# A two-block transformer on one core: attention scores of the first block in float32, or as a split into two float32r passes

## Chip, cores and metric

The kernel runs on one core of one Trainium2 chip. The metric is the device time of one execution in microseconds, the median of several runs.

## The reference, cut to what matters

The input is 256 tokens of width 1024. The first block has four layers: layer 0 and 3 use mixer A (16 query heads on 4 key heads, window 128, biases, sinks), layer 1 uses mixer B (three dilation groups of 16 heads each, merged by their softmax sums), layer 2 uses mixer C (16 heads, causal). Each layer is a mixer, an output projection, a layer norm, a gated feed-forward part and another layer norm. A second block of two layers follows (spatial gating, a state-space mixer, differential attention), which the change leaves as it is. All of it is float32. The scores of the first block come from

```python
s = jnp.einsum('bnqhgd,bnkhd->bnhgqk', qb, kb) * (dh ** -0.5)
...
m = s.max(-1)
p = jnp.exp(s - m[..., None])
l = p.sum(-1)
o = jnp.einsum('bnhgqk,bnkhd->bnqhgd', p, vb) / ...
```

with heads of 64 elements and blocks of 128 tokens; a query sees its own block and the one before it.

## The kernel before

The 256 tokens are two tiles of 128, and each tile is a *stream*: a Python generator that issues the projections of all layers in order. Beside the stream a tile has *tasks* (the attention of a finished projection, a hidden chunk of the feed-forward part), of which up to three advance at a time (`CONC`). `run` gives stream 0 a turn, then stream 1, which lags four turns (`LAG`). A turn lets each task go to its next `yield` and then issues one half unit of weights of the stream: two row blocks of the weights, three products each, so six products of 512 columns. `idle(n)` in a task waits n turns. This order and the dependences are all that orders the instructions on an engine; each engine works its own queue in order.

Every weight matrix is split: `load` fetches it (DMA on SP's queue), ScalarE makes the high part by a cast to float32r (line 396), VectorE the rest by a subtraction (line 400). `mm3` (lines 409 to 411) adds three float32r products: high by high, high by low, low by high. Activations are split in the same way after their transposes by TensorE (`blocks_t`, line 456; `split`, lines 447 and 448).

A projection chunk of 512 columns in layers 1 and 2 holds two blocks of 256 columns, that is four heads of queries, keys or values. `after` copies a block from PSUM to `stg` (line 765), rotates it (`rope_apply`, lines 581 to 584), and `heads_t` transposes it by TensorE and copies the result to SBUF by ScalarE (line 590). Then, a turn later, `attend` runs for the four heads: `scores` issues float32 products with 64 rows of contraction, two heads of different parity alternating between the upper and the lower 64 rows (line 614); VectorE adds the mask (lines 618 and 621) and finds the maxima (line 636), ScalarE takes exponentials (line 641); two turns later TensorE transposes them (line 664), and a turn after that come the products with the values (line 652). Layers 0 and 3 do the same in `keys` and `queries`; there each key head serves four query heads, and `keys` doubles the keys (line 711) so that both parities find them in their own 64 rows.

The first block calls `attend` 24 times for each token tile: 4 in each of layers 0, 2 and 3, 12 in layer 1. It handles 24 tiles of 256 query columns and 18 of key columns for each token tile. Tile 0 has 128 keys per head, tile 1 has 256. The second block's differential attention calls `scores` too.

`BUFS` gives the number of buffers of each kind of tile: here `tp` two PSUM banks for transposes, `v` values, `kt` and `qt` transposed keys and queries, `stg1` staged blocks, `ffg` the gates of the feed-forward part.

Of the kernel before, what the change touches and what calls it, by code (L numbers as in the profile page):

```python
# [9 lines left out]
F32 = mybir.dt.float32  # L10
# [57 lines left out]
W_QK_A = 1  # L68
W_QK_B = 0
W_SOFTMAX = 2  # L70
# [14 lines left out]
class Net:  # L85
# [45 lines left out]
    def own(self, name, shape, tag, dt=F32):  # L131

        if tag in ("s4", "yt", "lv", "cc", "cv", "xc", "sscb", "ssbt", "ssact"):
            self.second_pool()
        pp = self.pl if tag in ("ho", "wx", "yt") else self.pp
        return pp.tile([P] + shape, dt, name=name, tag=tag, bufs=BUFS[tag])
# [466 lines left out]

    def scores(self, t, q, k, mask):

        nc = self.nc
        nk = (t + 1) * P
        svs = [self.bank().rearrange("p (h k) -> p h k", k=256)[:, :, :nk] for _ in range(2)]  # L610
        for a in range(2):
            for j in range(t + 1):
                for par in range(2):
                    nc.tensor.matmul(svs[par][:, a, j * P:(j + 1) * P], q(par, a), k(par, a, j), start=True, stop=True)  # L614
        for sv in svs:
            if mask is None:
                m = self.mask["b0"][:, None, P:].to_broadcast([P, 2, P])
                nc.vector.tensor_add(sv[:, :, t * P:], sv[:, :, t * P:], m)
            else:
                m = mask[:, None, (1 - t) * P:].to_broadcast([P, 2, nk])  # L620
                nc.vector.tensor_add(sv, sv, m)
        return svs

    def attend(self, t, qt, kt, mask, v, sink=None):
# [6 lines left out]

        svs = self.scores(t, lambda par, a: qt[par * 64:par * 64 + 64, a, :],
                          lambda par, a, j: kt(j, par + 2 * a), mask)
        for par, sv in enumerate(svs):
# [50 lines left out]
    def mixer_a(self, t, i, xt, st):  # L685
# [13 lines left out]
        def keys(ps):  # L699
# [6 lines left out]
            self.rope_apply(z, 4, self.rope[1][t])  # L706

            k2 = []
            for a in range(2):
                k = self.own("k2", [2, 2, 64], "stg1")  # L710
                nc.vector.tensor_copy(k, z[:, 128 * a:128 * a + 128].rearrange("p (h d) -> p h d", d=64)[:, :, None, :]
                                      .to_broadcast([P, 2, 2, 64]))
                k2.append(k.rearrange("p h a d -> p (h a d)"))
            yield from self.idle(W_QK_A)
            st["k", t] = [self.heads_t(k, "kt", 1.0) for k in k2]

        def queries(c, ps):
# [7 lines left out]
            yield from self.idle(W_QK_A)  # L725
            qts = [self.heads_t(z, "qt", 0.125) for z in zs]
            yield
            def head(a):
                kvh = 2 * c + a
                h0 = 4 * kvh  # L730
                while ("k", 0) not in st:
                    yield
                o, nm = yield from self.attend(
                    t, qts[a], lambda jj, h: st["k", jj][kvh // 2][(h % 2) * 64:(h % 2) * 64 + 64, kvh % 2, :],
                    self.mask["a"], lambda jj, h: st["v", jj][:, kvh, :], nsk[:, h0:h0 + 4])
# [13 lines left out]
    def mixer_bc(self, t, i, xt, st, blocks, masks):  # L749
# [7 lines left out]
        def after(bl, ps):  # L757
# [12 lines left out]
            for z, what, qq, g in zs:  # L770
                if what == "k":
                    st["k", qq, g, t] = self.heads_t(z, "kt", 1.0)
                else:
                    qs.append((self.heads_t(z, "qt", 0.125), qq, g))
            if not qs:
                return
            yield
            for zt, qq, g in qs:
                while any((a, qq, g, j) not in st for a in "kv" for j in range(t + 1)):
                    yield  # L780
                o, nm = yield from self.attend(
                    t, zt, lambda j, h: st["k", qq, g, j][(h % 2) * 64:(h % 2) * 64 + 64, h // 2, :],
                    masks[g] and self.mask[masks[g]], lambda j, h: st["v", qq, g, j][:, h, :])
# [351 lines left out]
    def diff_attn(self, t, pr, st):  # L1135
# [7 lines left out]
        for hp in range(2):  # L1143
            ps, ls = [], []

            svs = self.scores(t, lambda m, a: qt[64 * m:64 * m + 64, 2 * hp + a, :],
                              lambda m, a, j: st["dk", j][64 * m:64 * m + 64, 2 * hp + a, :], None)
            for sv in svs:
# [374 lines left out]
```

## Time and profile before

| | us |
|---|---|
| median of 3 runs | 2391.38 |
| lowest and highest | 2390.16, 2392.42 |
| the profiled execution | 2393.47 |
| its span, first to last instruction | 2391.8 |
| TensorE busy | 2358.1 |
| VectorE busy | 1744.3 |
| ScalarE busy | 1314.9 |
| GpSimd busy | 124.7 |

PE is TensorE's products, PEld its weight loads, DVE VectorE, ACT ScalarE, POOL GpSimd, SP the engine that issues most DMAs. Products are pipelined: a record of a product lasts longer than its share of the engine (a product of 512 columns shows 0.39 us, but the next starts 0.23 us after it), so what a product costs is read from the steps in the chain or from the starts in the order of time. A line number can be that of a helper that many callers use. The granted clock of TensorE was at its full level (1.00, that is 2.4 GHz) in all four attention stretches.

### The profile page before, as it was taken

What the parts mean: (1) busy time and instruction counts of PE and PEld (TensorE: products, weight loads), DVE (VectorE), ACT (ScalarE), POOL (GpSimd) and SP (SyncE); (2) the same over time, 40 slices, a digit from 0 to 9 for tenths busy, and PEclk for the clock granted to TensorE, in tenths of its full rate; (3) what the DMA queues carried; (4) which work ended last, traced back from release to release, by engine and by line L of the source; (5) the groups of instructions that cost most, each with busy time, mean ns of one, the idle gap of its engine ahead of it and who ended that gap; (6) DMA issues with size and microseconds to landing.
All of it is one profiled execution on the core that took longest, in us unless ns stands there. A gap on an engine that the chain in (4) does not pass through costs nothing.

```text
span 2391.8 us, 34975 instructions
## 1 busy us (share of the span) xinstructions
PE 2358.1 (99%) x11664; PEld 1922.7 (80%) x11664; DVE 1744.3 (73%) x4282; ACT 1314.9 (55%) x2180; POOL 124.7 (5%) x411
## 2 busy tenths in 40 slices
PE   8999999999999999999999999999999999999999
PEld 6888888888888788887788877877888778788887
DVE  7765676666755767557775588987877889987876
ACT  5454456655544555444544445744677657545776
POOL 1000000000000000000000000100011201000111
PEclk9999999999999999999999999999999999999999
DMA  6366554444566635665366567467566686575653
GB/s 234 100 207 187 176 176 131 135 128 128 182 188 187 192 124 173 191 187 184 112 193 191 186 134 168 127 150 203 161 191 186 170 186 128 123 216 171 187 184 115
DMA packets 280117, 400.16 MB, mean 167 GB/s; under 512 B 20588, under 2 KB 205098, under 8 KB 279936
## 3 DMA queue, kind: packets, MB, share of 16 engines
q1 hardware_dynamic: 274784, 381.88, 55.4%
q0 software_dynamic: 5152, 16.05, 2.2%
q8 instruction: 92, 1.51, 0.3%
q14 instruction: 89, 0.73, 0.1%
HBM read 396.81 MB, written 1.05 MB: 166 GB/s over the span
## 4 chain that ended last, share of the span: by engine, by line
PE 87%; DVE 7%; DMA 3%; ACT 2%; issue 1%; SPq 0%; ACTq 0%; DVEq 0%
PE pj L409 21%; PE pj L411 21%; PE pj L410 21%; PE tp L456 4%; PE ch L409 4%; PE ch L411 4%; PE ch L410 4%; PE ch L614 3%; PE ch L652 3%; DVE w L400 2%; DMA raw<-in_w_in_dram 2%; PE tp L664 1%; ACT w L396 1%; DVE convy L1003 1%; DMA raw<-in_w_branch_c_dram 0%
## 5 line engine op out<-in xcount | busy, mean ns | idle before, releaser
L400 DVE TENSOR_TENSOR w<-raw,w 128x512 fp32r<-128x512 f32 x1456 | 956.3, 683 | 456.6 <-ACT w L396 455.1
L396 ACT CAST w<-raw 128x1024 fp32r<-128x1024 f32 x728 | 759.0, 1043 | 661.5 <-PE pj L411 361.0
L409 PE MATMUL pj<-w,xth 128*128 128x512 f32 x2048 | 821.7, 402 | 4.3 <-ACT w L396 1.6
L410 PE MATMUL pj<-w,xth 128*128 128x512 f32 x2048 | 806.1, 394 | 2.9 <-DVE w L400 2.9
L411 PE MATMUL pj<-w,xtl 128*128 128x512 f32 x2048 | 805.1, 394 | 0.7 <-DVE xtl L448 0.7
L409 PEld LDWEIGHTS pj<-w,xth 128*128 128x128 f32 x2048 | 386.4, 189 | 89.3 <-ACT xth L447 5.7
L411 PEld LDWEIGHTS pj<-w,xtl 128*128 128x128 f32 x2048 | 386.3, 189 | 85.4 <-DVE xtl L448 3.0
L410 PEld LDWEIGHTS pj<-w,xth 128*128 128x128 f32 x2048 | 386.9, 189 | 80.6 <-DVE w L400 5.3
L409 PE MATMUL ch<-w,fht 128*128 128x512 f32 x412 | 171.9, 417 | 1.8 <-ACT fht L447 1.8
L411 PE MATMUL ch<-w,fht 128*128 128x512 f32 x412 | 161.9, 393 | 0.0
L410 PE MATMUL ch<-w,fht 128*128 128x512 f32 x412 | 161.2, 391 | 0.0
L1003 DVE SCALAR_TENSOR_TENSOR convy<-xc,ffn_cw,convy 128x128 f32<-128x128 f32 x352 | 100.5, 345 | 7.1 <-POOL ffn_hist L994 2.1
L411 PEld LDWEIGHTS ch<-w,fht 128*128 128x128 f32 x412 | 77.3, 188 | 18.4 <-DVE fht L448 1.0
L409 PEld LDWEIGHTS ch<-w,fht 128*128 128x128 f32 x412 | 77.4, 188 | 15.5 <-ACT fht L447 3.9
L410 PEld LDWEIGHTS ch<-w,fht 128*128 128x128 f32 x412 | 77.9, 189 | 12.2
L641 ACT ACTIVATE pexp<-ch,nm 128x128 f32<-128x128 f32 (+1 forms) x192 | 65.9, 421 | 36.8 <-DVE nm L636 24.0
L845 ACT ACTIVATE ffg<-pj 128x256 f32<-128x256 f32 x88 | 33.9, 386 | 76.1 <-PE pj L411 76.0
L1000 ACT ACTIVATE convy<-xc,ffn_cw 128x128 f32<-128x128 f32 x176 | 72.8, 484 | 1.4
L652 PEld LDWEIGHTS ch<-v,pt 128*128 128x128 f32 x576 | 70.6, 191 | 2.9
L409 PE MATMUL pj<-w,fht 128*128 128x512 f32 x180 | 71.3, 396 | 0.0
L411 PE MATMUL pj<-w,fht 128*128 128x512 f32 x180 | 70.7, 393 | 0.0
L410 PE MATMUL pj<-w,fht 128*128 128x512 f32 x180 | 70.1, 389 | 0.0
(338 smaller groups left out, 2706.2 us busy)
## 6 DMA issues: line engine op xcount, KB each, us to landing
raw<-in_w_gate_up_dram SPq DMA_DIRECT2D x352, 256.0 KB, 3.3
raw<-in_w_in_dram SPq DMA_DIRECT2D x128, 512.0 KB, 5.0
raw<-in_w_down_dram SPq DMA_DIRECT2D x88, 512.0 KB, 3.6
raw<-in_ffn_w_up_dram SPq DMA_DIRECT2D x176, 256.0 KB, 3.3
raw<-in_b_w_qkv_dram SPq DMA_DIRECT2D x144, 256.0 KB, 3.1
raw<-in_ffn_w_down_dram SPq DMA_DIRECT2D x44, 512.0 KB, 4.4
raw<-in_a_w_qkv_dram SPq DMA_DIRECT2D x24, 512.0 KB, 4.5
raw<-in_c_w_qkv_dram SPq DMA_DIRECT2D x48, 256.0 KB, 3.1
```

Of the source, the lines that this page charges most:

```text
L396: nc.scalar.copy(w[:, 0, :m], raw)
L400: self.last_low = nc.vector.tensor_sub(w[:, 1, s], raw[:, s], w[:, 0, s].bitcast(F32)).ins
L409: mm(ps, xh[:, k, :], wh[:, kk, cols], start=start, stop=False)
L410: mm(ps, xh[:, k, :], wl[:, kk, cols], start=False, stop=False)
L411: self.last_mm = mm(ps, xl[:, k, :], wh[:, kk, cols], start=False, stop=stop).ins
L456: self.nc.tensor.transpose(tp[:, b * P:(b + 1) * P], src[:, b * P:(b + 1) * P], self.ident)
L614: nc.tensor.matmul(svs[par][:, a, j * P:(j + 1) * P], q(par, a), k(par, a, j), start=True, stop=True)
L641: nc.scalar.activation(p[:, a, :(t + 1) * P], sv[:, a, :], AF.Exp, bias=n2[:, a:a + 1])
L652: nc.tensor.matmul(o[:, par + 2 * a, :], pts[par][:, a * (t + 1) + j, :], v(j, par + 2 * a), start=j == 0, stop=j == t)
L845: nc.scalar.activation(g, ps[:, :FFC], AF.Silu)
L1000: nc.scalar.activation(y[:, a, :], xc[:, a, 4:], AF.Identity, bias=b[:, 0, c:c + 1], scale=w[:, h, c:c + 1])
L1003: nc.vector.scalar_tensor_tensor(y[:, a, :], xc[:, a, o:o + P], w[:, j, c:c + 1], y[:, a, :], op0=OP.mult, op1=OP.add)
```

## The change

The scores of the first block no longer multiply float32 operands of 64 rows. Queries and keys are split into a float32r high part and a float32r rest. A query tile holds the high part in the 64 rows of its head's parity and the rest in the other 64 rows; a key tile holds, for each parity, the high part in all 128 rows (`part` 0) and the rest in all 128 rows (`part` 1). One product over 128 rows then adds (high + rest of the query) times one part of the key, and two passes give the score. The high parts are written by ScalarE, the rests by VectorE, which writes the queries' rest across to the other 64 rows; for keys GpSimd copies both parts across. A key tile is shared by both token tiles, so a pass of token tile 1 takes 256 key columns at once. The doubled keys of layers 0 and 3 are no longer made by VectorE and transposed.

The scores are issued two turns after the transposes of their queries instead of one (`W_SPLIT`), in layers 1 and 2 the transposes a turn after the rotation instead of at once (`W_QK_B`), and in layer 1 the blocks come in the order keys, values, queries instead of values, keys, queries. Buffers: `v` 6 for 7; `ks` 2 and `qs` 3 in place of `kt` 5 and `qt` 3; `stg1` 6 takes in `ffg`. The second block keeps the old products under the name `scores_64`.

```diff
-            bc=3, bcs=1, v=7, kt=5, qt=3, stg1=2, og=7, ob=3, ffg=4,
+            bc=3, bcs=1, v=6, ks=2, qs=3, stg1=6, og=7, ob=3,
...
-W_QK_B = 0
+W_QK_B = 1
+W_SPLIT = 2
...
-                for w in (2, 1, 0):
+                for w in (1, 2, 0):
...
-    def heads_t(self, z, tag, scale):
-
+    def queries_t(self, z, scale):
+        nc = self.nc
         tp = self.blocks_t(z, 2)
-        zt = self.own("zt", [2, P], tag)
-        self.nc.scalar.activation(zt, tp, AF.Copy, scale=scale)
+        zt = self.own("zt", [2, 2, P], "qs", F32R)
+        for par in range(2):
+            here, there = self.half(par), self.half(1 - par)
+            nc.scalar.activation(zt[here, par], tp[here], AF.Copy, scale=scale)
+            nc.vector.scalar_tensor_tensor(zt[there, par], tp[here], scale, zt[here, par].bitcast(F32),
+                                           op0=OP.mult, op1=OP.subtract)
         return zt
+
+    def keys_t(self, z, ks, j):
+        nc = self.nc
+        tp = self.blocks_t(z, 2)
+        s = slice(j * P, (j + 1) * P)
+        for par in range(2):
+            here, there = self.half(par), self.half(1 - par)
+            nc.scalar.copy(ks[here, 0, par, :, s], tp[here])
+            nc.vector.tensor_sub(ks[here, 1, par, :, s], tp[here], ks[here, 0, par, :, s].bitcast(F32))
+            nc.gpsimd.tensor_copy(ks[there, :, par, :, s], ks[here, :, par, :, s])
...
+    def key_pair(self):
+        return self.own("ks", [2, 2, 2, 2 * P], "ks", F32R)
...
+    def scores(self, t, q, k, mask):
+        svs = self.score_banks(t)
+        for par, sv in enumerate(svs):
+            for a in range(2):
+                for part in range(2):
+                    self.nc.tensor.matmul(sv[:, a, :], q(par, a), k(par, a)[:, part, :(t + 1) * P],
+                                          start=part == 0, stop=part == 1)
+        return self.masked(t, svs, mask)
...
-            k2 = []
-            for a in range(2):
-                k = self.own("k2", [2, 2, 64], "stg1")
-                nc.vector.tensor_copy(k, z[:, 128 * a:128 * a + 128].rearrange("p (h d) -> p h d", d=64)[:, :, None, :]
-                                      .to_broadcast([P, 2, 2, 64]))
-                k2.append(k.rearrange("p h a d -> p (h a d)"))
             yield from self.idle(W_QK_A)
-            st["k", t] = [self.heads_t(k, "kt", 1.0) for k in k2]
+            self.keys_t(z, self.shared((i, "ks"), self.key_pair), t)
...
-            qts = [self.heads_t(z, "qt", 0.125) for z in zs]
-            yield
+            qts = [self.queries_t(z, 0.125) for z in zs]
+            yield from self.idle(W_SPLIT)
...
-                    st["k", qq, g, t] = self.heads_t(z, "kt", 1.0)
+                    self.keys_t(z, self.shared((i, "ks", qq, g), self.key_pair), t)
...
-                    qs.append((self.heads_t(z, "qt", 0.125), qq, g))
+                    qs.append((self.queries_t(z, 0.125), qq, g))
...
-            yield
+            yield from self.idle(W_SPLIT)
...
-        g = self.own("ffg", [FFC], "ffg")
+        g = self.own("ffg", [FFC], "stg1")
```

## Rows read from the trace of the kernel before

**Rows 1.** The page, part 1: busy time, share of the span, instructions.

```profile
PE 2358.1 (99%) x11664; PEld 1922.7 (80%) x11664; DVE 1744.3 (73%) x4282; ACT 1314.9 (55%) x2180; POOL 124.7 (5%) x411
```

**Rows 2.** The page, part 4: the chain that ended last, by engine.

```profile
PE 87%; DVE 7%; DMA 3%; ACT 2%; issue 1%; SPq 0%; ACTq 0%; DVEq 0%
```

**Rows 3.** Busy time by stretch: length, engines, PEclk, DMA share, GB/s.

```profile
30.00:100.00 70.00, 67.47 (x419) 54.84 (x417) 54.27 (x166) 39.30 (x88) 3.13 (x8) 1.00 0.41 129
...
300.00:620.00 320.00, 319.70 (x1835) 262.89 (x1835) 221.50 (x603) 185.68 (x391) 3.67 (x26) 1.00 0.45 137
...
815.00:925.00 110.00, 109.96 (x633) 90.64 (x632) 72.55 (x193) 65.18 (x128) 0.59 (x4) 1.00 0.44 137
...
1125.00:1195.00 70.00, 69.67 (x409) 55.28 (x407) 56.27 (x167) 40.02 (x89) 1.59 (x3) 1.00 0.40 131
```

**Rows 4.** TensorE's waits in 300 to 620 us: total, times, longest.

```profile
PE pj L411 <- DVE ho L448: 0.3, 1, 0.3
```

**Rows 5.** The chain by lines, for 30:100, 300:620, 815:925 and 1125:1195.

```profile
by line: PE ch L614 15.6%; PE ch L652 14.6%; PE pj L409 11.7%; PE pj L411 10.9%; PE pj L410 10.7%; PE tp L664 7.7%; PE tp L456 5.2%; DVE w L400 4.7%; ACT pexp L641 3.1%; ACT w L396 3.0%; issue 2.9%; DVE x L857 1.6%; PE ch L409 1.3%; PE ch L
...
by line: PE pj L409 23.9%; PE pj L411 22.5%; PE pj L410 22.1%; PE ch L652 9.6%; PE ch L614 7.8%; PE tp L664 4.9%; PE tp L456 4.3%; DMA raw<-in_w_gate_up_dram 1.2%; DVE w L400 0.6%; DVE x L553 0.4%; DVE xtl L448 0.4%; PE ch L411 0.4%; PE ch 
...
by line: PE pj L409 24.3%; PE pj L410 22.1%; PE pj L411 22.0%; PE ch L652 9.3%; PE ch L614 7.6%; PE tp L456 6.0%; PE tp L664 4.8%; PE ch L409 1.5%; PE ch L411 1.3%; PE ch L410 1.3%; issue 0.0%
...
by line: PE pj L409 19.1%; PE pj L411 17.4%; PE ch L614 17.4%; PE pj L410 17.4%; PE ch L652 9.8%; PE tp L456 8.1%; PE tp L664 8.0%; PE ch L409 0.9%; PE ch L410 0.7%; PE ch L411 0.7%; ACT zt L590 0.6%; issue 0.2%
```

**Rows 6.** Line 614: its products, ns min/median/max, first and last start.

```profile
L614 PE MATMUL ch<-zt x576: 272/272/373, 39.1 to 1189.8; 64*128 64x128 f32 x192
```

**Rows 7.** The chain in order of time, 430 to 437 us: start, us, what.

```profile
431.38 0.23 PE pj L411
431.62 0.65 PE ch L614 x8
432.26 0.43 PE pj L409
...
433.85 1.46 PE ch L614 x15
435.31 0.43 PE pj L409
```

**Rows 8.** TensorE in order of time around line 1108: start, us, instruction.

```profile
1583.86 0.40 PE L410 MATMUL pj<-w,xth 128*128 128x512 f32 x1
1584.09 0.56 PE L1108 MATMUL ch<-ssact,pick 128*128 128x128 f32 x4
1584.49 0.44 PE L411 MATMUL pj<-w,xtl 128*128 128x512 f32 x1
1584.77 0.39 PE L409 MATMUL pj<-w,xth 128*128 128x512 f32 x1
```

**Rows 9.** Groups by line and shape, VectorE and ScalarE: count, busy, mean ns, idle before.

```profile
L448 DVE TENSOR_TENSOR fht<-tp,fht 128x256 fp32r<-128x256 f32 x104 | 43.5, 418 | 1.1 <-ACT fht L447 1.1
L1072 DVE TENSOR_TENSOR ssact<-ch,ssact 64x128 fp32r<-64x128 f32 x4 | 1.2, 294 | 0.1
L711 DVE COPY k<-stg 128x256 f32<-128x256 f32 x8 | 2.3, 284 | 0.1
L590 ACT ACTIVATE zt<-tp 128x256 f32<-128x256 f32 x88 | 32.0, 386 | 34.2 <-PE tp L456 33.1 <-PE ch L614 0.8 <-ACT zt L590 0.2
```

**Rows 10.** Groups by line: copies on GpSimd, and VectorE beside them.

```profile
L166 POOL COPY maskt<-same 128x128 f32<-128x128 f32 x2 | 0.6, 292 | 31.7 <-DVE same L220 31.7
L1473 POOL COPY tick<-x 128x1 f32<-128x1 f32 x1 | 0.2, 189 | 2.3 <-DMA x<-in_x_dram 2.3
L994 POOL COPY ffn_hist<-xc 128x2 f32<-128x2 f32 x88 | 28.1, 364 | 466.5 <-ACT xc L990 466.5
L1003 DVE SCALAR_TENSOR_TENSOR convy<-xc,ffn_cw,convy 128x128 f32<-128x128 f32 x352 | 100.5, 345 | 7.1 <-POOL ffn_hist L994 2.1 <-ACT convy L1000 1.4
```

**Rows 11.** Busy time from 75 to 80 us, columns as in rows 3.

```profile
75.00:80.00 5.00, 4.75 (x42) 4.34 (x41) 1.87 (x9) 0.92 (x4) 0.20 (x1) 1.00 0.40 133
```

More of the change, by code (lines that the diff above doesn't have):

```diff
@@ L134, in own @@
             self.second_pool()
-        pp = self.pl if tag in ("ho", "wx", "yt") else self.pp
+        pp = self.pl if tag in ("ho", "wx", "ks", "yt") else self.pp
         return pp.tile([P] + shape, dt, name=name, tag=tag, bufs=BUFS[tag])
@@ L602, in v_tile, with masked @@
         return v
-    def scores(self, t, q, k, mask):
+    def masked(self, t, svs, mask):
         nc = self.nc
-        nk = (t + 1) * P
-        svs = [self.bank().rearrange("p (h k) -> p h k", k=256)[:, :, :nk] for _ in range(2)]
-        for a in range(2):
-            for j in range(t + 1):
-                for par in range(2):
-                    nc.tensor.matmul(svs[par][:, a, j * P:(j + 1) * P], q(par, a), k(par, a, j), start=True, stop=True)
         for sv in svs:
@@ L619, in scores, with score_banks, scores_64 @@
             else:
-                m = mask[:, None, (1 - t) * P:].to_broadcast([P, 2, nk])
+                m = mask[:, None, (1 - t) * P:].to_broadcast([P, 2, (t + 1) * P])
                 nc.vector.tensor_add(sv, sv, m)
         return svs
+    def score_banks(self, t):
+        return [self.bank().rearrange("p (h k) -> p h k", k=256)[:, :, :(t + 1) * P] for _ in range(2)]
+    def scores(self, t, q, k, mask):
[6 more added lines that the diff above has]
+        return self.masked(t, svs, mask)
+    def scores_64(self, t, q, k):
+        svs = self.score_banks(t)
+        for a in range(2):
+            for j in range(t + 1):
+                for par in range(2):
+                    self.nc.tensor.matmul(svs[par][:, a, j * P:(j + 1) * P], q(par, a), k(par, a, j),
+                                          start=True, stop=True)
+        return self.masked(t, svs, None)
     def attend(self, t, qt, kt, mask, v, sink=None):
@@ L630, in attend @@
         ps = []
-        svs = self.scores(t, lambda par, a: qt[par * 64:par * 64 + 64, a, :],
-                          lambda par, a, j: kt(j, par + 2 * a), mask)
+        svs = self.scores(t, lambda par, a: qt[:, par, a, :], lambda par, a: kt(par + 2 * a), mask)
         for par, sv in enumerate(svs):
@@ L706, in keys @@
             self.rope_apply(z, 4, self.rope[1][t])
-            k2 = []
-            for a in range(2):
-                k = self.own("k2", [2, 2, 64], "stg1")
-                nc.vector.tensor_copy(k, z[:, 128 * a:128 * a + 128].rearrange("p (h d) -> p h d", d=64)[:, :, None, :]
-                                      .to_broadcast([P, 2, 2, 64]))
-                k2.append(k.rearrange("p h a d -> p (h a d)"))
             yield from self.idle(W_QK_A)
-            st["k", t] = [self.heads_t(k, "kt", 1.0) for k in k2]
+            self.keys_t(z, self.shared((i, "ks"), self.key_pair), t)
+            st["k", t] = True
         def queries(c, ps):
@@ L780, in after @@
                     yield
+                ks = self.shared((i, "ks", qq, g), None)
                 o, nm = yield from self.attend(
-                    t, zt, lambda j, h: st["k", qq, g, j][(h % 2) * 64:(h % 2) * 64 + 64, h // 2, :],
+                    t, zt, lambda h: ks[:, :, h % 2, h // 2, :],
                     masks[g] and self.mask[masks[g]], lambda j, h: st["v", qq, g, j][:, h, :])
@@ L1144, in diff_attn @@
             ps, ls = [], []
-            svs = self.scores(t, lambda m, a: qt[64 * m:64 * m + 64, 2 * hp + a, :],
-                              lambda m, a, j: st["dk", j][64 * m:64 * m + 64, 2 * hp + a, :], None)
+            svs = self.scores_64(t, lambda m, a: qt[64 * m:64 * m + 64, 2 * hp + a, :],
+                                 lambda m, a, j: st["dk", j][64 * m:64 * m + 64, 2 * hp + a, :])
             for sv in svs:
```

7 lines of the change are left out of this document (6 added, 1 removed).

## The prediction

> **What bounds the kernel now.** The first part of the page comes first: TensorE is busy 99% of the span, VectorE 73%, ScalarE 55%, GpSimd 5% [rows 1]. A busy share alone does not say that an engine sets the pace, so the chain that ended last is read next: 87% of it is TensorE, 7% VectorE, 2% ScalarE [rows 2]. Third, the four stretches in which the first block computes attention, taken stage by stage: layer 0 at 30 to 100 us, layer 1 (three dilation groups, most of the scores) at 300 to 620, layer 2 at 815 to 925, layer 3 at 1125 to 1195. There VectorE is busy 78%, 69%, 66% and 80% (busy time over the length of the stretch) [rows 3]. In layer 1 TensorE's waits for other engines come to 0.3 us in 320 [rows 4]. So layers 1 and 2 cost exactly what TensorE's instructions cost, one after the other; in layers 0 and 3 VectorE stands close behind.
>
> **What the scores cost now.** The chain by lines gives line 614 15.6% of 70 us in layer 0, 7.8% of 320 in layer 1, 7.6% of 110 in layer 2, 17.4% of 70 in layer 3 [rows 5]: 10.9 + 25.0 + 8.4 + 12.2 = 56.4 us. That is for 576 passes [rows 6]: the code has 288 float32 products here (96 for token tile 0, 192 for tile 1), so each is two passes, over 64 rows.
>
> A run of scores costs more than its own line shows. In the pieces of the chain a run of 8 passes takes 0.65 us, and the projection product behind it 0.43 us in place of 0.23: 0.85 in all. A run of 15 or 16 takes 1.46 + 0.20 [rows 7]. I counted 66 runs in TensorE's order of time, from 39.1 to 1189.8 us, the first and last starts of the row (13, 29, 8 and 16 by layer). At 0.20 us each they add 13.2 us, so scores now cost **69.6 us**.
>
> **What they will cost.** An attend call makes 8 passes whichever tile it is: 2 head parities x 2 x 2 parts, of 128 moving columns for tile 0 and 256 for tile 1. There are 24 calls per tile (4 in each of layers 0, 2, 3 and 12 in layer 1). The nearest row for 128 columns is line 1108, whose operands are float32r: four passes between two projection products. From line 410 at 1583.86 to line 409 at 1584.77 is 0.91 us; two ordinary steps of 0.23 leave 0.45, or 0.113 each [rows 8]. For 256 columns no row exists. The low end is 0.113; the high end 0.23, the step of 512 columns [rows 7]. I take 0.12, nearest to the row of few columns, since half of 0.23 is 0.115 too. So 24 x 8 x 0.113 + 24 x 8 x 0.12 = 21.7 + 23.0 = **44.7 us**; at the high end, 66 us. All is on full 128 rows, so I drop the 0.20 per run; line 1108 pays none.
>
> Saving by layer, with 0.90 + 0.96 for a pair of calls: layer 0, 10.9 + 2.6 - 7.4 = 6.1; layer 1, 25.0 + 5.8 - 22.3 = 8.5; layer 2, 8.4 + 1.6 - 7.4 = 2.6; layer 3, 12.2 + 3.2 - 7.4 = 8.0. Layers 0 and 3 also lose the doubled keys: 8 transposes, at line 1108's 0.113 about 0.9 us. TensorE's work falls by **26 us**.
>
> A rule speaks against this. The Trainium skill, TensorEngine Tiling (Array Packing), section Overview, says that a contraction of 64 rows can run as two independent tiles, up to twice as fast, and the change gives that up. The trace agrees only in some runs: 8 passes in 0.65 us is 0.081 each, but 15 in 1.46 is 0.097 [rows 7]. Were every run as well packed as the first, the old scores would be 576 x 0.081 + 13.2 = 60 us and TensorE would save 16 us, not 26.
>
> **What the split adds.** Per token tile 24 query and 18 key tiles, 84 in all. Each now takes two ScalarE and two VectorE instructions of 64 partitions x 256 elements, where it took one ScalarE copy of 128 x 256. VectorE took 0.42 us for 128x256 from PSUM and 0.29 for 64x128 [rows 9]; half the partitions save little, and I take 0.42 (low end 0.29). ScalarE: 0.39 more each, 19 us on 186 in layer 1, which leaves it at two thirds; hidden. VectorE gets 48 x 2 x 0.42 = 40.3 us in layer 1, 13.4 in layer 2, and in layers 0 and 3 each 8.4, less four copies of keys at 0.28 [rows 9], +7.3.
>
> Against the stages as TensorE would leave them: layer 1, 221.5 + 40.3 = 262 of 311 us, 84%; layer 2, 72.6 + 13.4 = 86 of 107, 80%; layer 0, 54.3 + 7.3 = 61.6 of 63.4, 97%; layer 3, 56.3 + 7.3 = 63.6 of 61.5, **103%**. So layers 0 and 3 can't have their saving whole. VectorE would be what is late next there. With VectorE at 93% (an estimate between today's 80% and the full stretch), they end at 66.2 and 68.4 us: 3.8 and 1.6 us won. Layers 1 and 2 keep 11.1, less some 1.5 us of new waits (an estimate; now 0.3).
>
> **GpSimd** gets 72 copies of 64 x 512 elements. 128 elements took 0.29 us there and one took 0.19 [rows 10], so about 0.6 each, 29 us in layer 1, where it is nearly idle. A copy waits for VectorE's subtraction; queued behind it are the ones-column of the next values and the small parameter loads of line 511. Scores need the copy six turns later, each turn pair at least twelve projection passes of 0.23 = 2.8 us [rows 7]: hidden. If that cover went, a key would cost its 0.6.
>
> **Edits with one answer.** The later scores (two turns, and one more ahead of layer 1 and 2's transposes) lengthen the way of a head, not TensorE's work: the other token tile's projections fill it, except in layers 0 and 3, where it is in VectorE's slack above. Keys ahead of values, six value buffers for seven, two key buffers and the merged staging buffers: nothing, as a buffer's last reader stands at least two turns before its next writer. No SP transfer is moved. The second block keeps its scores.
>
> **The sum**: 3.8 + 1.6 + 11.1 - 1.5 = 15 us, from a span of 2391.8. The profiled execution took 2393.47, 1.7 more, and the median of the timed runs is 2391.38; I subtract from the median: **2376 us**, own range 2370 to 2384.
>
> **Rivals.**
> *VectorE keeps up in layers 0 and 3.* At 0.29 us a split the total there is 60 us of 63 and the whole 26 us would come through: 2365. For it: from 75 to 80 us VectorE is busy 1.87 us of 5 [rows 11], slack that later work could fill. Chance 0.17.
> *VectorE becomes the bound in layer 1 too.* If GpSimd's copies also hold VectorE, layer 1 gets 29 us more: 291 of 311, 93%, the level at which I let layers 0 and 3 clip; little is left but 2 us: 2389. Against it: line 1003 takes 345 ns beside 88 history copies, while those copies of two elements take 364 against 189 for a lone one [rows 10]: GpSimd waits, VectorE doesn't. Chance 0.16. The Trainium skill, SBUF — State Buffer, section Who interferes with whom, calls the port that the two share an exclusive lock, held by whichever came first; the trace agrees so far that something holds GpSimd, but shows no long GpSimd copy that could hold VectorE.
> *The two transpose banks.* A split holds its PSUM bank for two ScalarE and two VectorE instructions (two of 0.39 and the last 0.42, about 1.2 us, more behind other work in VectorE's queue) instead of 0.39; TensorE's next transposes stand in order behind. It decides from 26 / 84 = 0.31 us of waiting per split; at 0.45 it costs 38 - 26 = 12 us: 2403, slower. Against it: the hidden tiles' split already holds a bank over a VectorE instruction 104 times [rows 9], and TensorE's waits show nothing. Chance 0.13.
> *A pass of 256 columns isn't cheap.* At 0.23 the saving is 26 - 21 = 5: 2386. Chance 0.04.
>
> **How the numbers follow.** Forecast 0.50. The range takes in all but the bank rival: 2363 to 2393. A measurement of this kernel can tell about 0.2%, 5 us, from no change: faster is below 2386.6. Forecast, first rival and half of the last: with a little of the second, 0.72; within, 0.14; slower, 0.14.
>
> **What would show it.** Score runs of 8 passes at 0.90 and 0.96 us, with the projection product behind them back near 0.23; VectorE at 84% in layer 1 and above 90% in layers 0 and 3; GpSimd copies near 0.6 us. Wrong if TensorE waits for the split lines or for transposes by more than a few us in layer 1, or if the passes of 256 columns take 0.2.

## The result, and the profile after

The changed kernel takes **2415.26 us** (median of 4 runs, 2412.29 to 2417.79) beside 2391.74 for the kernel before on the same chip: a ratio of 1.0099, 95% interval 1.0081 to 1.0116. It is 1% slower, outside the range given. The profiled execution took 2415.1 us with a span of 2413.4. Line numbers from here on are those of the changed kernel: 410 to 412 the three products of `mm3` (409 to 411 before), 401 the rest of the weights on VectorE (400 before), 653 the scores (614), 685 the exponentials (641), 708 their transposes (664), 696 the products with the values (652), 457 the transposes in `blocks_t` (456). New are 596 and 597 (queries: high part, rest) and 609, 610, 611 (keys: high part, rest, GpSimd's copy).

The page's busy times, as [rows 1] have them for the kernel before:

```profile
PE 2352.2 (97%) x11464; PEld 1924.1 (80%) x11464; DVE 1814.7 (75%) x4442; ACT 1343.3 (56%) x2260; POOL 189.0 (8%) x483
```

TensorE has 200 instructions fewer and VectorE 70 us more, as the diff says. But TensorE's busy time fell by 6 us while the span grew by 22: TensorE now stands still. Where, the stretches tell (columns as in [rows 3], with one stretch more, behind layer 1's attention):

```profile
30.00:100.00 70.00, 62.44 (x342) 52.18 (x342) 58.68 (x174) 40.48 (x94) 6.43 (x10) 0.90 0.36 115
300.00:620.00 320.00, 313.04 (x1713) 259.16 (x1711) 255.15 (x685) 202.56 (x438) 45.67 (x74) 1.00 0.44 135
...
600.00:700.00 100.00, 94.69 (x458) 78.05 (x457) 68.26 (x141) 46.92 (x71) 1.47 (x6) 0.97 0.53 163
...
1125.00:1195.00 70.00, 64.18 (x323) 50.20 (x321) 67.25 (x194) 38.11 (x75) 6.39 (x8) 1.00 0.49 156
```

TensorE was idle 2.5 us of 70 in layer 0 and 0.3 of 320 in layer 1; now it is idle 7.6 and 7.0. The clock column is new too: 0.90 in layer 0, 0.97 behind layer 1, where it was 1.00. The kernel before in the stretch behind layer 1:

```profile
600.00:700.00 100.00, 99.38 (x464) 80.94 (x463) 67.73 (x139) 47.64 (x67) 1.27 (x4) 1.00 0.60 183
```

TensorE's waits in 300 to 620 us (before: 0.3 us in all, [rows 4]):

```profile
PE ch L653 <- ACT pexp L685: 2.3, 4, 0.6
PE tp L457 <- DVE zt L597: 1.3, 3, 0.5
PE tp L708 <- DVE zt L597: 1.0, 4, 0.2
PE tp L457 <- DVE ob L719: 0.8, 2, 0.4
```

The first is for the three PSUM banks called `ch`, which hold scores until their exponentials are read.

The new scores themselves, TensorE in order of time (compare [rows 7]):

```profile
445.11 1.00 PE L653 MATMUL ch<-ks,zt 128*128 128x128 f32 x8
445.95 0.45 PE L410 MATMUL pj<-w,xth 128*128 128x512 f32 x1
446.23 0.40 PE L411 MATMUL pj<-w,xth 128*128 128x512 f32 x1
...
608.78 1.11 PE L653 MATMUL ch<-ks,zt 128*128 128x256 f32 x8
609.73 0.38 PE L457 MATMUL tp<-ident,ob 128*128 128x128 f32 x2
```

The kernel before, behind a run of eight, and its next run:

```profile
432.19 0.50 PE L409 MATMUL pj<-w,xth 128*128 128x512 f32 x1
432.53 0.39 PE L410 MATMUL pj<-w,xth 128*128 128x512 f32 x1
...
433.78 1.53 PE L614 MATMUL ch<-zt 64*128 64x128 f32 x16
435.24 0.50 PE L409 MATMUL pj<-w,xth 128*128 128x512 f32 x1
```

Eight passes of 128 columns take 0.84 us from start to start, eight of 256 take 0.95, and the product behind the former 0.28 in place of 0.34. (The 0.43 in [rows 7] is counted along the chain and also holds some 0.1 us lost ahead of the run.) The operations that the split adds, by line and shape (compare [rows 9, 10]):

```profile
L611 POOL CAST ks<-ks 64x512 fp32r<-64x512 f32 x72 | 65.1, 904 | 303.3 <-DVE ks L610 301.9
...
L597 DVE SCALAR_TENSOR_TENSOR zt<-tp,zt 64x256 fp32r<-64x256 f32 x96 | 38.5, 420 | 9.8 <-ACT zt L596 7.4
...
L596 ACT ACTIVATE zt<-tp 64x256 fp32r<-64x256 f32 x96 | 35.3, 378 | 18.2 <-DVE zt L597 12.2 <-PE tp L457 3.8
...
L610 DVE TENSOR_TENSOR ks<-tp,ks 64x256 fp32r<-64x256 f32 x72 | 30.2, 420 | 10.3 <-ACT ks L609 8.7
```

**The end of layer 1** is the largest single piece. First the kernel before, then the changed one, from the last scores to the output projection:

```profile
595.69 1.16 PE L614 MATMUL ch<-zt 64*128 64x128 f32 x16
604.61 1.89 PE L652 MATMUL ch<-v,pt 128*128 128x65 f32 x16
608.68 0.40 PE L456 MATMUL tp<-ident,ob 128*128 128x128 f32 x2
```

```profile
617.77 1.84 PE L696 MATMUL ch<-v,pt 128*128 128x65 f32 x15
624.77 0.66 PE L457 MATMUL tp<-ident,ob 128*128 128x128 f32 x2 [5.16 <-DVE ob L719]
...
626.49 0.63 PE L411 MATMUL pj<-w,ho 128*128 128x512 f32 x1
626.91 0.63 PE L412 MATMUL pj<-w,ho 128*128 128x512 f32 x1
627.34 0.63 PE L410 MATMUL pj<-w,ho 128*128 128x512 f32 x1
```

The last scores of token tile 1 started at 595.69 and now start at 608.78, the products with the values come 13 us later too, and when they are done no projection is left: TensorE waits 5.16 us for the last head group's output `ob`. Much of the wait is VectorE's queue: the last heads' merging and division are four instructions, 1.4 us in all, but they take from 620.05 to 624.63, among subtractions of weights and a layer norm. The first and the last of the four:

```profile
620.05 0.43 DVE L852 TENSOR_TENSOR og<-og,eg 128x260 f32<-128x260 f32 x1 [0.34 <-ACT og L829]
...
624.21 0.42 DVE L719 TENSOR_TENSOR ob<-og,rl 128x256 f32<-128x256 f32 x1
```

After the wait the products stand 0.43 us apart instead of 0.23. The granted clock there (column 7, behind the length and five engines):

```profile
624.70:630.00 5.30, 5.23 (x19) 4.07 (x20) 2.17 (x4) 1.45 (x3) 0.00 (x0) 0.65 0.48 143
```

0.65 as a mean over a stretch that changes from the 1.2 GHz level to the 2.4 GHz level.

**A count by products.** All kernels here issue 8688 projection products on TensorE, the same number in every stage. How far a kernel is behind when it starts the k-th of them tells in which stage the time goes. These are differences against the kernel before in us, worked out from the starts in the two traces, each kernel's profiled execution:

| kernel | end of layer 0's attention (k=240) | layer 1, all but its end (1920) | end of layer 1 (2060) | layer 2 (3260) | layer 3 (4200) | median |
|---|---|---|---|---|---|---|
| changed | 5.2 | 8.4 | 16.3 | 21.8 | 21.7 | 2415.3 |
| e1 all turns and order, no split | 4.4 | 8.2 | 16.4 | 22.6 | 26.1 | 2416.1 |
| e7 two turns, no split | 4.4 | 7.7 | 15.6 | 18.6 | 22.5 | 2413.0 |
| e14 e7, not for the last heads | -1.2 | 3.4 | 4.1 | 6.7 | 5.2 | 2397.5 |
| e8 transposes a turn later, no split | 0.0 | -3.4 | 4.1 | 5.8 | 5.6 | 2397.5 |
| e15 e8, not for the last heads | 0.0 | -0.6 | -0.4 | 0.0 | -0.1 | 2391.5 |
| e2 split, old turns, new order | 2.1 | 8.7 | 8.4 | 9.6 | 11.3 | 2404.2 |
| e9 split, old turns and order | 1.8 | 5.7 | 5.4 | 6.8 | 8.2 | 2400.7 |
| e10 e9 without the subtractions | -0.2 | -0.9 | -1.1 | -1.5 | -4.0 | 2390.0 |
| e12 e9 with one score bank for tile 0 | 1.7 | 4.1 | 5.2 | 6.8 | 7.4 | 2398.3 |
| e13 e10 with one score bank for tile 0 | 0.7 | -4.3 | -4.7 | -5.2 | -7.8 | 2385.8 |
| e6 new order of blocks only | 1.9 | 2.3 | 2.0 | 1.9 | 1.9 | 2392.3 |

The last row shows how far the table can be trusted: e6's layer 0 is the kernel before's own code, yet that execution stands 1.9 us behind there (its granted clock in 30 to 100 us is 0.98), and keeps this through the four layers. So differences under some 2 us say nothing. The profiled executions also lie up to 3 us from the medians: the kernel before's took 2393.47, e12's 2401.23, the slowest of its runs. And inside a layer a kernel with later turns looks too good by the work of the heads that it has put behind the k-th product; only at a layer's end is all of it done.

Behind these products come layer 3's feed-forward part and the second block, which all kernels have alike; there none of them moves by more than some 3 us.

### The profile page after: what moved, and what is told of

Same layout as the page of the kernel before. It is cut to its first block, busy times and chain, and to the rows that moved or that the text cites. A ratio compares the mean times of both kernels' runs of the same rounds, so it can differ in the third digit from the quotient of the medians.

```text
span 2413.4 us, 35003 instructions
## 1 busy us (share of the span) xinstructions
PE 2352.2 (97%) x11464; PEld 1924.1 (80%) x11464; DVE 1814.7 (75%) x4442; ACT 1343.3 (56%) x2260; POOL 189.0 (8%) x483
## 4 chain that ended last, share of the span: by engine, by line
PE 52%; DVE 8%; DMA 2%; ACT 2%; issue 1%; ACTq 0%; SPq 0%; DVEq 0%
PE pj L410 13%; PE pj L412 13%; PE pj L411 13%; PE ch L410 3%; PE ch L412 3%; PE ch L411 3%; PE tp L457 3%; DVE w L401 2%; DMA raw<-in_w_in_dram 1%; ACT w L397 1%; PE ch L696 1%; PE tp L708 1%; DVE convy L1044 1%; DMA raw<-in_w_branch_b_dram 0%; DMA lam<-in_da_lambda_dram 0%
## 5 line engine op out<-in xcount | busy, mean ns | idle before, releaser
L410 PEld LDWEIGHTS ch<-w,fht 128*128 128x128 f32 x412 | 77.5, 188 | 15.5 <-ACT fht L448 3.9
L611 POOL CAST ks<-ks 64x512 fp32r<-64x512 f32 x72 | 65.1, 904 | 303.3 <-DVE ks L610 301.9
L685 ACT ACTIVATE pexp<-ch,nm 128x128 f32<-128x128 f32 (+1 forms) x192 | 65.9, 427 | 39.8 <-DVE nm L680 22.6
L457 PE MATMUL tp<-ident,stg 128*128 128x128 f32 x424 | 71.1, 279 | 5.3 <-DVE zt L597 2.9
L457 PEld LDWEIGHTS tp<-ident,stg 128*128 128x128 f32 x424 | 50.9, 141 | 28.4 <-ACT pt L710 6.8
```

Source lines behind the costliest of these rows:

```text
L410: mm(ps, xh[:, k, :], wh[:, kk, cols], start=start, stop=False)
L457: self.nc.tensor.transpose(tp[:, b * P:(b + 1) * P], src[:, b * P:(b + 1) * P], self.ident)
L611: nc.gpsimd.tensor_copy(ks[there, :, par, :, s], ks[here, :, par, :, s])
L685: nc.scalar.activation(p[:, a, :(t + 1) * P], sv[:, a, :], AF.Exp, bias=n2[:, a:a + 1])
```

## The experiments

Two theories stood at the start: that the later turns cost the time, since heads come late where nothing else is left to do; and that the split costs it, by its work on VectorE and GpSimd.

**The turns, without the split.** e1_turns_alone gives the kernel before all three changes of order; e7_two_turns_alone, e8_late_transposes_alone and e6_order_alone one each.

```diff
-W_QK_B = 0
+W_QK_B = 1
+W_SPLIT = 2
...
-                for w in (2, 1, 0):
+                for w in (1, 2, 0):
...
-            yield
+            yield from self.idle(W_SPLIT)
```

> The kernel before with only the change's order: W_QK_B 1, two turns between the transposes of the queries and their scores, keys ahead of values; the float32 scores and the single copies stay. The changed kernel took 2415.3 us against 2391.7, and counted by projection products it falls behind by 5.2 us in layer 0, 3.2 in the body of layer 1, 8 at its end, 1.5 in the body of layer 2, 4 at its end and nothing later. Theory A (the later turns leave the last heads of a layer without other work beside them): the ends of layers 1 and 2 and some of layer 0 show up here too, about +12 us, 2404. Theory B (the split's own work on VectorE and ScalarE, and the transpose banks that it holds): no difference, 2391 to 2393.

2416.07 us (2415.91 to 2418.37), ratio 1.0108 (1.0091 to 1.0125): 25 us slower with the old scores. The theory that the turns cost time is right in kind; the price is twice what it gave.

e7, the two turns only (`W_SPLIT`, both uses):

> The kernel before with two turns instead of one between the queries' transposes and their scores, nothing else. Theory A with the blame on this turn: layer 0 +4, the end of layer 1 +4 to +8, the end of layer 2 +3, layer 3 +3, in all 2403 to 2410. With the blame on the other turn (the transposes a turn later): +2 to +6, in layers 0 and 3 alone.

2412.98 us, 1.0089 (1.0069 to 1.0110): 21 us more, above the range given. By the table 4.4 of it is in layer 0, 11 in layer 1 and about 3 and 4 in layers 2 and 3. TensorE's longest waits in e7, in 30 to 115 and in 595 to 660 us, are both for the last heads; in the kernel before the first is 0.4 us and the second isn't there:

```profile
PE tp L665 <- ACT pt L667: 3.6, 1, 3.6
...
PE tp L457 <- DVE ob L676: 3.5, 1, 3.5
```

e8, `W_QK_B = 1` only:

> The kernel before with W_QK_B 1, that is the transposes of layers 1 and 2 a turn after the rotation, nothing else; layers 0 and 3 don't use it and should not change. Blame on this turn: the body of layer 1 +4 (its transposes meet those of the exponentials at the two transpose banks) and 4 to 8 at the ends of layers 1 and 2, 2400 to 2403. Blame on the other: under +3.

2397.50 us (7 runs), 1.0025 (1.0014 to 1.0036): 6 us more, between the two forecasts. At the 1920th product it is 3.4 us ahead, and then the end of layer 1 costs 7.5. The 3.4 are not a gain: in the kernel before TensorE waits 0.3 us in 320 here [rows 4], and e8 has the same instructions, so the lead is work of heads that it has yet to do. Over layer 1 the price is 4.1.

e6, the order of the blocks only:

> The kernel before with the blocks of layer 1 in the order keys, values, queries, nothing else. The three edits of order together cost 25 us (2416 against 2391). Theory A (the later turns cost it): no difference here, 2390 to 2393. Rival (the order of blocks costs it, as it moves which blocks share a chunk): most of the 8 us at the end of layer 1 and the 4 us in its body, and nothing in layers 0, 2 and 3.

2392.29 us, 1.0003 (0.9993 to 1.0014): nothing.

**The split, in the old turns.** e2_turns_undone sets `W_QK_B` and `W_SPLIT` in the changed kernel back; e9_split_alone takes the order back too.

```diff
-W_QK_B = 1
-W_SPLIT = 2
+W_QK_B = 0
+W_SPLIT = 1
...
-                for w in (1, 2, 0):
+                for w in (2, 1, 0):
```

> The changed kernel with W_QK_B 0 and W_SPLIT 1, the turns of the kernel before; split scores, order of blocks and buffers stay. Theory A: the ends of layers 1 and 2 go back to what they were, about -12 us, 2403. Theory B: 2415, or slower, up to 2425, as the scores then wait for a split that has a turn less.

2404.19 us (2403.01 to 2405.71), 1.0056 (1.0041 to 1.0071), near theory A's 2403: beside the split the turns cost 11 us.

> The changed kernel with all three edits of order undone: the split scores in the order and turns of the kernel before. With the turns alone undone it took 2404, 13 us over the kernel before, of which TensorE waited 6 us for score banks (for the exponentials) in layer 1. Theory C (the split's VectorE instructions stand between the scores and their maxima in VectorE's queue, so the three score banks come free later): the same waits, 2400 to 2406. Rival (the new order of blocks brings the scores of both token tiles together): without it the waits go and TensorE's saving shows, 2378 to 2391.

2400.68 us (5 runs), 1.0037 (1.0022 to 1.0051). So the split by itself costs 10 us where 15 were to be won, as theory C has it. The end of layer 1 is back to normal; by the table 1.8 us are lost in layer 0, 3.6 in layer 1 and 1.4 in each of layers 2 and 3. The largest part is inside layer 1. VectorE and its neighbours in e2, from a run of scores to its exponentials:

```profile
437.53 0.41 DVE L639 TENSOR_TENSOR ch<-ch,mask_b 128x256 f32<-128x256 f32 x1
437.67 0.61 POOL L611 CAST ks<-ks 64x512 fp32r<-64x512 f32 x1 [12.41 <-DVE ks L610]
437.86 0.96 DVE L401 TENSOR_TENSOR w<-raw,w 128x512 fp32r<-128x512 f32 x1
438.85 0.43 DVE L610 TENSOR_TENSOR ks<-tp,ks 64x256 fp32r<-64x256 f32 x1
439.31 0.43 DVE L639 TENSOR_TENSOR ch<-ch,mask_b 128x256 f32<-128x256 f32 x1
...
439.77 0.76 DVE L680 TENSOR_REDUCE nm<-ch 128x2 f32<-128x256 f32 x2
440.29 0.88 ACT L685 ACTIVATE pexp<-ch,nm 128x128 f32<-128x128 f32 x3 [2.17 <-DVE nm L680]
440.44 0.68 DVE L401 TENSOR_TENSOR w<-raw,w 128x512 fp32r<-128x512 f32 x1
```

and TensorE at the same place:

```profile
436.15 1.00 PE L653 MATMUL ch<-ks,zt 128*128 128x128 f32 x8
...
441.01 0.71 PE L653 MATMUL ch<-ks,zt 128*128 128x256 f32 x4 [1.48 <-ACT pexp L685]
```

The same tile and group in the kernel before:

```profile
431.55 0.72 PE L614 MATMUL ch<-zt 64*128 64x128 f32 x8
...
433.47 1.14 ACT L641 ACTIVATE pexp<-ch,nm 128x128 f32<-128x128 f32 x4 [0.77 <-DVE nm L636]
```

From the first score to the first exponential it was 1.9 us and is now 4.1: between the mask of one parity and that of the other VectorE works off a subtraction of weights, 0.96 us long beside a GpSimd copy (0.68 without one), and the rest of a key. Token tile 1's second bank of scores can't be written before token tile 0's exponentials have freed one, so TensorE stands for 1.48 us, the longest of four such waits in 295 to 598 us:

```profile
PE ch L653 <- ACT pexp L685: 6.0, 4, 1.5
```

**How much of that is VectorE, how much GpSimd.** In the changed kernel, e4_dve_twice does each of the 168 subtractions twice, e5_pool_twice each of the 72 copies:

```diff
+            nc.vector.scalar_tensor_tensor(zt[there, par], tp[here], scale, zt[here, par].bitcast(F32),
+                                           op0=OP.mult, op1=OP.subtract)
...
+            nc.vector.tensor_sub(ks[here, 1, par, :, s], tp[here], ks[here, 0, par, :, s].bitcast(F32))
```

> The changed kernel with each of the split's 168 VectorE subtractions issued twice (same result): some 70 us more of VectorE work in the first block. Theory A: little, under +6 us. Theory B, by VectorE's load or by the banks held: at least as much again as the bodies of the stages lost against the forecast, +10 to +30 us, most of it in the bodies of layers 1 and 2.

2430.32 us (2 runs), 1.0165 (1.0144 to 1.0185): 15 us over the changed kernel, for 168 x 0.42 = 71 us more on VectorE. That is theory B.

```diff
+            nc.gpsimd.tensor_copy(ks[there, :, par, :, s], ks[here, :, par, :, s])
```

> The changed kernel with each of GpSimd's 72 key copies issued twice: they take 0.90 us each, so 65 us more on GpSimd. Theory A: no difference (under 3 us). Theory B in the form that GpSimd's copies hold VectorE or that scores wait for keys: +5 us or more, and VectorE's subtractions of weights longer on average than 688 ns.

2419.06 us (2 runs), 1.0118 (1.0097 to 1.0138): 4 us over it, between the two forecasts, and the intervals of the two kernels overlap. VectorE's subtractions of weights took 688 ns in the mean, as in the changed kernel, so theory B's sign isn't there.

e10_split_without_vector is e9 with no subtraction at all; it leaves the rests out, which lie in fixed tiles of zeros:

```diff
-        zt = self.own("zt", [2, 2, P], "qs", F32R)
+        zt = self.fixed("qs", [2, 2, P])
...
-            nc.vector.scalar_tensor_tensor(zt[there, par], tp[here], scale, zt[here, par].bitcast(F32),
-                                           op0=OP.mult, op1=OP.subtract)
...
-            nc.vector.tensor_sub(ks[here, 1, par, :, s], tp[here], ks[here, 0, par, :, s].bitcast(F32))
```

> The split scores in the turns and order of the kernel before (2400.7 as it stood), but without VectorE's 168 subtractions: the rests of queries and keys stay zero, written once; ScalarE's copies, GpSimd's copies and TensorE's passes are all there, so the scores are those of the high parts alone. Theory C (the subtractions stand in VectorE's queue between scores and maxima, and the three score banks come free later): TensorE's waits for score banks in layer 1 (4.4 us) go, and the saving in passes shows at last: 2370 to 2382. Rival (ScalarE's halves, GpSimd's copies or the transpose banks do it): 2394 to 2401.

2390.04 us (10 runs), 0.9994 (0.9984 to 1.0003): neither theory's number. The subtractions are worth 2400.68 - 2390.04 = 10.6 us. But the shorter passes bring nothing clear of noise even without them: TensorE still waits for score banks. Its waits in 295 to 598 us:

```profile
PE ch L671 <- ACT pexp L703: 5.3, 6, 1.0
```

**An earlier way out that wasn't one.** e11_keys_later takes e9 and splits the keys of a chunk that also holds queries two turns later, in a task of their own, so that VectorE has the queries first.

```diff
-                if what == "k":
+                if what == "k" and len(zs) > 1:
+                    self.spawn(t, late_keys(z, qq, g))
+                elif what == "k":
```

> The split scores in the turns and order of the kernel before, with the keys of a chunk that also holds queries transposed and split two turns later, by a task of their own; nothing is left out. The keys have six turns to spare. Theory C: half of the subtractions no longer fall between scores and maxima, the waits for score banks in layers 1 and 2 shrink to a third, 2393 to 2398. Rival (VectorE's load as such): 2400 to 2402.

2415.79 us, 1.0104 (1.0087 to 1.0121): a miss. TensorE's waits in 295 to 660 us show 4.5 us for `ob` at the end of layer 1, and keys that came too late (2.7 us for GpSimd's copies):

```profile
PE tp L458 <- DVE ob L720: 4.5, 1, 4.5
PE ch L654 <- POOL ks L612: 2.7, 11, 0.4
```

The first is the changed kernel's own wait. That the extra task takes one of the three places, so that the heads behind it start later, is the likely reason; it isn't shown.

**The score banks.** In e9 and in e10, token tile 0's four heads (4 x 128 columns) now go into one bank instead of two, with one mask and one maximum.

```diff
+        if t == 0:
+            b = self.bank().rearrange("p (h k) -> p h k", k=P)
+            svs = [b[:, par::2, :] for par in range(2)]
...
+            m = (self.mask["b0"] if mask is None else mask)[:, None, P:].to_broadcast([P, 4, P])
+            self.nc.vector.tensor_add(b, b, m)
...
+            nc.vector.tensor_reduce(nm, b, axis=AX.X, op=OP.max, negate=True)
```

> This is the split alone (order and turns of before, 2400.7 us) with one edit: token tile 0's four heads put their 4 x 128 columns of scores into one bank instead of two, so one add of the mask and one maximum serve it instead of two of each, and the two token tiles together hold exactly the three score banks. Theory D (what takes the gain of the shorter passes is the third score bank, which comes free only after the exponentials of the scores before): TensorE's waits for score banks in layer 1, 5 us in the split alone, fall under 2 us, VectorE's work falls by 24 x 2 short operations, and the time falls by 5 to 9 us to 2392-2396. Rival E (the wait is VectorE's lateness itself, and a bank more changes nothing, since the single mask add now waits for all eight passes and both halves' exponentials come later): 2399-2403, with the waits as before or at the transposes instead.

2398.26 us (6 runs), 1.0029 (1.0018 to 1.0041): 2.4 us under e9, which the intervals don't separate, just below the rival's range and short of theory D's.

> The kernel with the split but without VectorE's subtractions (2390.0 us; it leaves out the low rests of queries and keys, so the scores are those of the high parts alone), with token tile 0's scores in one bank as in the run before. Theory D (banks): the 5 us of waits for score banks that this kernel still has in layer 1 go, and the saving of the shorter passes shows at last: 2376-2384, 6 to 14 us under it. Rival E (the waits are not for want of a bank; what remains has another place, the transposes or the chain through the exponentials): 2387-2392.

2385.81 us (7 runs), 0.9974 (0.9963 to 0.9986): 4.2 us under e10 and 5.2 under the kernel before, between the two forecasts. Yet the wait itself did what theory D says. First e9, then e12, then e13, in 295 to 598 us:

```profile
PE ch L653 <- ACT pexp L685: 4.4, 6, 0.8
...
PE ch L653 <- DVE zt L597: 0.7, 2, 0.4
```

```profile
PE ch L654 <- DVE zt L597: 2.8, 8, 0.4
```

```profile
PE tp L736 <- ACT pt L738: 1.1, 2, 0.6
```

With a bank to spare no score of layer 1 waits for exponentials. In e12 part of the wait goes over to VectorE's rests of the queries; in e13, without these, it goes, and layer 1 is at last 5.4 us shorter than before (by the table, 0.7 behind at its start, 4.7 ahead at its end). That is the saving of the passes, seen where little stands in its way. In layer 0 even e13 wins nothing: in 28 to 112 us TensorE waits for

```profile
PE pj L410 <- DVE stg L788: 2.3, 1, 2.3
PE tp L736 <- ACT pt L738: 1.6, 1, 1.6
PE ch L672 <- ACT pexp L713: 1.5, 1, 1.5
```

a staged projection, transposed exponentials and a score bank; in the kernel before the first two are 1.3 and 0.4 us and the third isn't there.

**The last heads.** e14_two_turns_not_last is e7 with one turn for the last heads of each layer, e15_late_not_last is e8 likewise. In layers 1 and 2 that is the last quarter; in layers 0 and 3 `c == 0` is the first of two chunks, so in e14 it is the last half, and not the quarter of its expectation. `W_QK_B` is used in layers 1 and 2 alone, so layer 3, which e15's expectation names too, stays as it was.

```diff
-            yield from self.idle(W_SPLIT)
+            yield from self.idle(W_SPLIT if c == 0 else 1)
...
-            yield from self.idle(W_SPLIT)
+            yield from self.idle(1 if qs[-1][1] == 3 else W_SPLIT)
...
-            yield from self.idle(W_QK_B)
+            yield from self.idle(0 if bl[-1][2] == 3 else 1)
```

> The kernel before with scores two turns behind their transposes (2413.0 us so), except in the last quarter of the heads of each layer of the first block, where it stays at one. Theory F (what the two turns cost at the ends of layers comes from the last heads, which find no projections left beside them): the 8 us at the end of layer 1, 4 in layer 0, 3 and 4 at the ends of layers 2 and 3 go, the 3 to 4 us inside layer 1 stay: 2394-2399. Rival G (the price belongs to the length of the way itself; a shorter last way only moves it, since the heads before are late all the same and the last stand behind them): 2406-2413.

2397.45 us (9 runs), 1.0023 (1.0014 to 1.0033), within theory F's range: of e7's 21 us 15.5 are gone. The wait for `ob` is gone. The end of layer 1 costs 0.7 us instead of 8, and the stretch behind it is as before:

```profile
600.00:700.00 100.00, 98.93 (x462) 80.10 (x460) 67.98 (x138) 47.42 (x66) 1.26 (x4) 1.00 0.59 180
```

> The kernel before with the transposes of layers 1, 2 and 3 one turn later (2397.5 us so), except in the last quarter of each layer. Theory F: the 7.5 us at the end of layer 1 and the 1.8 us at the end of layer 2 go, the 3.4 us that it wins inside layer 1 stay: 2386-2390. Rival G: 2394-2398, the gain given back later in the layer.

2391.45 us (11 runs), 1.0002 (0.9993 to 1.0011): a little above theory F's range. The ends cost nothing, as it has it. Of a lead of 2.8 us at the 1400th product only 0.6 is left at the 1920th, and the time is the kernel before's: the work put off is done there, and nothing was won by putting it off.

e16_one_bank_late puts the same later transposes into e12.

> The split alone with token tile 0's scores in one bank (2398.3 us) and the transposes one turn later except in the last quarter of each layer. If the later transposes win their 3 us inside layer 1 beside the split too: 2393-2396, the best kernel with the split, still not under the kernel before. If the split's waits (TensorE's scores for VectorE's rests of queries) are made worse by it: 2398-2402.

2398.80 us (8 runs), 1.0031 (1.0020 to 1.0041), in the second of the two ranges: no gain over e12, as e15 has none over the kernel before. No whole kernel with the split came under the kernel before.

## Why the prediction was wrong, point by point

**The step that failed** stands in "Edits with one answer": the later scores "lengthen the way of a head, not TensorE's work: the other token tile's projections fill it". They fill it only while there are projections. At the end of a layer both tiles have issued theirs, the output projection needs the last heads, and TensorE stands until they come: 5.16 us in the changed kernel, 3.5 in e7, not at all in e14. The step was priced at nothing. The two turns cost 21 us alone (e7), 15.5 of them through the last heads of each layer (e14). The exception that I made for layers 0 and 3 was priced with VectorE's slack, the wrong engine: e7 has no split, and layer 0 loses 4.4 us in it.

**What the wait brings with it** was not in any term. Behind the wait of 5.16 us the granted clock is 0.65 over 5.3 us, with products 0.43 us apart: at most 0.35 x 5.3 = 1.9 us of lost work. Layer 0's 70 us at a mean of 0.90 are at most 7 us, but not all of that need be the change's, as e6 has 0.98 there without any. How much of the price it is can't be told more closely from these runs.

**The passes** were sized rightly: 0.84 and 0.95 us against 0.90 and 0.96, and the product behind those of 128 columns is at 0.28, so of the 0.20 per run that was dropped 0.05 is still there. **The saving of 26 us** that I made of it was not. It takes each pass saved for time saved, which holds only where TensorE's own work is what sets the time. That was read from waits of 0.3 us in layer 1, but this figure tells what the old passes waited for, not how soon a shorter one could start. In layer 1 about half of the shorter passes' time was given back in front of the next scores, at the three banks: of 8.5 us forecast e10 wins 0.9 and e13, with a bank free, 5.4. Over the whole kernel e13 wins 5.2 of 26 by the medians. In layers 0 and 3 I took VectorE as the limit; without its subtractions layer 0 still wins nothing and layer 3 2.6 of 8.0. TensorE's waits in e13's layer 0 are for a staged projection on VectorE as well as for exponentials; which of them sets the time there is not shown.

**VectorE's price** was mis-sized in layers 1 and 2. The 0.42 us was right to the digit, and busy shares of 80% in layer 1 and 96% in layer 3 are near the 84% and "above 90%" given; layer 0, at 84%, falls short. But I priced the new waits in layers 1 and 2 at 1.5 us because the engine has slack on average. It works off its queue in order, and in the rows of e2 subtractions stand between the scores and their maxima: 10.6 us by e10, 6.3 of them in layers 1 and 2 by the table, and 15 by e4 for as many again.

**The rivals.** The two transpose banks came nearest in time (2403; the split alone, e9, has 2401) but not in place: waits for `tp` on the split's line 597 are 2.3 us in layer 1 of the changed kernel, 0.05 for each of the 48 splits there, where 0.31 were needed to take the whole saving, and TensorE's longest waits there are for the score banks. VectorE as the bound in layer 1 did not happen (80%). GpSimd's copies do hold it in places (the row of 0.96 us in e2), but its subtractions of weights take 688 ns in the mean against 683, and twice the copies cost no more than 4 us. Keys ahead of values cost nothing, as said (e6). The rule of the Trainium skill on two tiles of 64 rows (TensorEngine Tiling (Array Packing), section Overview) would have taken 10 us from a saving of 26; as most of it never came, no run here tells. The run of 15 in 1.46 us that the prediction set beside it has 16 passes in TensorE's order of time (433.78 to 435.24), so 0.091 each and not 0.097.

**The two prices don't add.** Turns 25 and split 10 make 24 together. Beside the split the turns cost 11 (the changed kernel against e2), and TensorE's waits for score banks in 295 to 598 us are 2.3 us with the new turns and 6.0 with the old ones. That the queries' rests and the keys have longer until the scores need them would explain it; that is argued, not shown.

**What stays open.** Two turns also cost 3.4 us inside layer 1, where projections are at hand (e14), and TensorE's waits there are too short to account for it. Between the 480th and the 1992nd product (counted in the two traces as in the table) e14 changes from projections to other work 130 times, the kernel before 112 times, and from start to start, idle time left out, e14's projection products take 364.2 us in all instead of 360.4. That is the size of it; why the later turn breaks the projections up more was not tried. The smaller buffers were never tried alone; e10 and e13 have them too and are not slower than the kernel before. Nor was the split tried with two turns everywhere but at the ends of layers, or with its subtractions elsewhere than on VectorE.

## What to carry to other kernels

Before a step is moved later, look at the last item of each stage and not at the middle: write down what TensorE still has to do between the moved step and the first reader of the stage's result, and price the lateness there in full. An engine without waits is not yet an engine whose saved time is saved: ask which buffer the next of the shortened operations needs, and when that comes free. And price work added to an in-order engine by what stands behind it in the queue, whatever its busy share.

## What the hardware showed that was not expected

GpSimd's copies of 64 x 512 elements took 0.61 us in the row of e2, which began ahead of a subtraction of weights, and 0.90 in the mean of the changed kernel. VectorE's subtraction of weights, 0.68 us as a rule, took 0.96 when it began 0.19 us after such a copy and 0.42 before its end. In the kernel before, GpSimd alone seemed to wait [rows 10]. The Trainium skill, SBUF — State Buffer, section Who interferes with whom, has the shared port as an exclusive lock. The traces now agree in both directions, with 0.28 us for VectorE in that row and 0.29 in the mean for GpSimd.

TensorE's wait of 5.16 us for `ob` was followed by products 0.43 us apart instead of 0.23, and the granted clock in those 5.3 us is 0.65 in the mean. In the kernel before, no attention stretch of the first block had less than 1.00 [rows 3].

Passes of 128 and of 256 columns over 128 rows cost nearly the same, 0.105 and 0.119 us (0.84 and 0.95 by 8): twice the columns for 13% more.
